# A gated attention trunk: the feed-forward input multiplied by tokens, the residual kept by features

## The chip, the cores and the metric

The kernel runs on one core of a Trainium2 chip. Its five engines work from queues of their own: TensorE (PE in the profile, with PEld for its weight loads), VectorE (DVE), ScalarE (ACT), GpSimd (POOL) and SyncE (SP), which here issues nearly all DMA transfers. The metric is the device time of one execution in microseconds, the median of the runs; smaller is better.

A matmul on TensorE holds one operand of 128 x 128 (the stationary one, `lhsT` in the code) and streams the other (the moving one, `rhs`, up to 512 columns) against it. The profile names a matmul as output <- moving, stationary.

## The reference

Two layers over 512 tokens of 1,024 features, float32. Each adds a gated mixture of a pooling mixer and a differential attention to the residual, and then a SwiGLU feed-forward:

```python
for i in range(DEPTH):                                  # DEPTH = 2
    xn = rmsnorm(x, norm1_g[i])
    u_pool, q, k, v, g_a, g_b = split(xn @ w_in[i])     # 1024 -> 6 x 1024
    q = rotary(rmsnorm(q, q_norm_g[i])); k = rotary(rmsnorm(k, k_norm_g[i]))
    o = diff_attention(q, k, v, lam)                    # softmax(qk, 0) - lam * softmax(qk, 1), chunk-causal
    attn_out = rmsnorm(o, subln_g[i]) * (1 - lam_init)
    pool_out = pool_mixer(u_pool, pool_w[i], pool_scale[i])
    x = x + (sigmoid(g_a) * pool_out + sigmoid(g_b) * attn_out) @ w_out[i]
    hn = rmsnorm(x, norm2_g[i])
    gate, up = split(hn @ w_ffn_in[i])                  # 1024 -> 2 x 2816
    x = x + (silu(gate) * up) @ w_ffn_out[i]            # 2816 -> 1024
```

`rmsnorm(x, g)` is `x * rsqrt(mean(x * x) + 1e-6) * g` over the features of a token.

## The kernel before

**Precision.** Every large product is done in three matmuls. An operand is split into a high part, rounded to the type that TensorE takes, and a low part, the rest; high x high, high x low and low x high are summed in PSUM (`product`, L277 to L285). Weights come in pieces of 512 KB (`piece`, `loaded`) and are split on arrival: a cast on ScalarE (L198) and a subtraction on VectorE (L199). `parts` has a second way: cast, negative copy, and a DMA from memory that adds the weights onto it (L236 to L238, issued by POOL). Raw pieces rotate through 7 buffers, split ones through 6 pairs.

**Layout.** The residual `res` lies by tokens, four tiles of 128 tokens by 1,024 features. A norm (`normed`, L346) squares a tile on ScalarE, raises the mean to the power -1/2 on POOL, scales by it and by the gains on VectorE, and then turns the tile into features by tokens with eight transposes on TensorE (L303); the split of these is the moving or stationary operand of what follows. Layer 0's first norm is different: its input also comes transposed from the host, the products are made of unnormalized `x * g`, and 1/rms is applied behind them (`token_stats`, `spread_rms`). Sums over features are made there with eight small matmuls against a column of ones (L471).

**Mixers.** Four heads, one after the other: query and key, value and gate, then the pooling branch and `merged`, whose last step is a product with the pool weights, two multiplications on VectorE (L750, L751) and a split (L204, L205). Probabilities, queries and outputs are turned by blocks of 32 on VectorE (L310), written to memory by one DMA and read back by four (`turned`, L306 to L316), all on SP's queue. The output projection adds into `res` as heads finish, and the last two heads are projected together (`project_out(..., True)`).

**Feed-forward.** The input product of a pair of hidden tiles, gate and up, 512 columns in all, is made by Strassen's scheme in Winograd's form: the weights are cut into four quarters (half of the features by gate or up), the activations likewise (half of the features by 256 tokens), and seven products replace eight. Sums of weight quarters are made per pair on VectorE (`Ffn.sums`, L816 to L830), sums of activation quarters once per layer (`Quarters`). A product is 24 matmuls (`pair_product`, L287 to L300): weights are held, 256 columns of tokens move. SwiGLU follows by features (`swiglu`). There are 11 pairs in a layer; after 8, 16 and 22 tiles their output product adds into `res` (`ffn_out`), hidden held and weights moving 512 wide, four tiles of tokens by two column blocks.

**Order.** The program is written as one stream. Steps that need a result of another engine are put off by a due time, counted in moving columns (`later`, `run_due`, with the constants `NORM_WAIT`, `QK_AWAY` and so on), and are written into the stream when the matmul count has reached it. The framework's planner then orders each engine's instructions by that stream and by its own estimate of times, hands out buffers by tag, and sets the semaphores; `tc.issue_after` fixes an order by hand.

Of the kernel before, what the change touches and what calls it, by code (L numbers as in the profile page):

```python
# [18 lines left out]
P = 128  # L19
# [20 lines left out]
ROUNDS = ((0, 8), (8, 16), (16, 22))  # L40
# [4 lines left out]
HIDDEN_AT = {0: "u", 2: "m", 4: "pr", 6: "us", 8: "mj", 10: "u", 12: "m", 14: "pr", 16: "us", 18: "u", 20: "m"}  # L45
# [3 lines left out]
QK_AWAY, SCORE_AWAY, PROB_AWAY, AV_AWAY, MERGE_AWAY = 28000, 26000, 32000, 18000, 24000  # L49


def weight_plan():
# [3 lines left out]
    def block(name, layer, cols, k0=0, k1=KD):  # L56
        for k in range(k0, k1, 2):
            plan.append((name, layer, k, 2, cols))
# [12 lines left out]

    for layer in range(L):
        def out(heads):
            for cb in range(2):
                for j in heads:
                    block("w_out", layer, span((512 * cb, 512)), 2 * j, 2 * j + 2)

        for i, j in enumerate(ORDER):
            block("w_in", layer, qk(j))
            if i >= 2:  # L80
                out(ORDER[i - 2:i - 1])
# [4 lines left out]
        out(ORDER[2:])  # L86

        def ffn_in(f, parts):
            cols = span((P * f, 256)), span((FF + P * f, 256))
            for k, up in parts:  # L90
                plan.append(("w_ffn_in", layer, k, 4, cols[up]))

        def ffn_out(f0, f1):
            for cb in range(2):
                block("w_ffn_out", layer, span((512 * cb, 512)), f0, f1)

        for part in ((0, 0), (4, 0)):
            for f in (0, 2):
                ffn_in(f, (part,))
        for r, (f0, f1) in enumerate(ROUNDS):  # L100
            for f in range(f0, f1, 2):
                ffn_in(f, ((0, 0), (0, 1), (4, 1), (4, 0))[1 if f < 4 else 0:3 if f < 4 else 4])
                if r and f == f0:
                    ffn_out(*ROUNDS[r - 1])
        ffn_out(*ROUNDS[-1])
# [4 lines left out]
def trunk_kernel(  # L110
    ctx: ExitStack,
    tc: tile.TileContext,
    x: bass.AP,
# [3 lines left out]
    gains: bass.AP,  # L117
# [31 lines left out]
    stats = const.tile([P, 5, NT], F32, name="stats")  # L149
    mhalf = const.tile([P, 4], F32, name="mhalf")  # L150
    scale = const.tile([P, L * KD + KD], F32, name="scale")
    neglam = [const.tile([P, 1], F32, name=f"nl{i}") for i in range(L)]
    l2s = [const.tile([P, 2], F32, name=f"l2{i}") for i in range(L)]
    const.tile([P, 40], F32, name="pad2")
# [3 lines left out]
    for tag, width, bufs in (("ss", 1, 4), ("r", 4, 4), ("ss4", 4, 4), ("st", 2, 4), ("mx", 2, 4), ("rc", 2, 4), ("sso", 1, 4),  # L158
                             ("head", 16, 2)):
# [3 lines left out]
    res = [sb.tile([P, D], F32, name=f"res{t}", tag=f"res{t}") for t in range(NT)]  # L163
# [43 lines left out]
    def piece(raw=None):  # L207
        i = at[0]
        at[0] += 1
        if raw is None:  # L210
            raw = sb.tile([P, 2, 512], F32, name="raw", tag="raw", bufs=RAWS)
        transfers.append(nc.sync.dma_start(raw.rearrange("p a b -> p (a b)"), wts[i]))
        hi = sb.tile([P, 2, 512], F32R, name="whi", tag="whi", bufs=SPLITS)
        lo = sb.tile([P, 2, 512], F32R, name="wlo", tag="wlo", bufs=SPLITS)
        split(hi, lo, raw)
        return [(hi[:, a, :], lo[:, a, :]) for a in range(2)]

    def loaded():
# [3 lines left out]
        raw = sb.tile([P, 4, VD], F32, name="raw", tag="raw", bufs=RAWS)  # L222
        nc.sync.dma_start(raw.rearrange("p a b -> p (a b)"), wts[i])
        return i, raw

    def tiles(x):
        return [x[:, k, :] for k in range(x.shape[1])]

    def parts(src, piece_no=None):
# [817 lines left out]
```

## Time and profile before

| | |
|---|---|
| median of 3 runs | 1408.1 us (1407.98 to 1408.12) |
| span of the profiled execution | 1406.2 us |
| instructions in it | 21,911, of them 8,140 matmuls |
| DMA | 203.21 MB in 109,979 packets, 145 GB/s on average |
| loads of weight pieces | 244 on SP's queue, 60 more that add onto a split part on POOL's |
| round trips through memory (`turned`) | 84 writes, 336 reads |

The profile is of one execution. A page line gives an engine's busy time, its share of the span and its instructions. A row of the groups view reads: line, engine, operation, output <- inputs, shapes, count | busy us, mean ns of one | idle time of the engine before them and what ended it. A row of the windows view gives for a stretch its length, then busy time and count of each engine, the granted clock and the DMA engines' share and rate. A row of the timeline gives start, duration, engine, line, operation and count of equal neighbours.

### The profile page before, as it was taken

The page shows a single profiled execution, that of the slowest core. Times are in us where ns is not written, and L with a number is a line of the kernel's source. Part 1 is how long each engine was busy: PE and PEld are TensorE (multiplying, and loading weights), DVE is VectorE, ACT ScalarE, POOL GpSimd, SP SyncE. Part 2 cuts the span into 40 slices and gives each one's busy share as a digit, 9 for nine tenths or more (in the row PEclk, how much of TensorE's full clock was granted, in tenths as well). Part 3 has the DMA queues.
Part 4 walks back from the last instruction along what each step waited for, and adds up shares of the span by engine and source line. Part 5 has one row for each costly group of instructions (what it writes and reads, how often), then busy time and mean ns, then how long its engine had stood idle before and what let it go on. Part 6 is the DMA issues. An engine that isn't in the chain of part 4 may idle for free.

```text
span 1406.2 us, 21911 instructions
## 1 busy us (share of the span) xinstructions
PE 1399.6 (100%) x8140; PEld 1237.5 (88%) x8140; DVE 1023.0 (73%) x1923; ACT 688.2 (49%) x1309; POOL 119.0 (8%) x144
## 2 busy tenths in 40 slices
PE   9999999999999999999999999999999999999999
PEld 7888888888999899989888888888889998999897
DVE  7779788697998558737577887767769974676462
ACT  6554343444766346425354543435447662563350
POOL 1010000100000001000010001000010000010000
PEclk9999999999999999999999999999999999999999
DMA  9344453453368357628334445435524682585351
GB/s 363 106 128 136 136 162 122 132 156 103 92 166 225 104 128 187 181 60 236 110 134 151 145 132 175 135 119 155 173 48 127 163 228 68 150 187 158 98 143 60
DMA packets 109979, 203.21 MB, mean 145 GB/s; under 512 B 37424, under 2 KB 62512, under 8 KB 109872
## 3 DMA queue, kind: packets, MB, share of 16 engines
q1 hardware_dynamic: 99936, 168.24, 37.1%
q0 software_dynamic: 8640, 31.46, 12.5%
q10 hardware_dynamic: 1296, 2.11, 0.6%
q8 instruction: 64, 1.05, 0.3%
q14 instruction: 43, 0.35, 0.1%
HBM read 184.07 MB, written 17.69 MB: 143 GB/s over the span
## 4 chain that ended last, share of the span: by engine, by line
PE 97%; DVE 1%; DMA 1%; POOL 0%; issue 0%; ACT 0%; DVEq 0%; SPq 0%; POOLq 0%
PE mm L282 20%; PE mm L284 19%; PE mm L283 19%; PE mm L296 6%; PE mm L294 6%; PE mm L297 6%; PE sc L294 3%; PE sc L297 3%; PE sc L296 3%; PE tr L297 2%; PE tr L294 2%; PE tr L296 2%; PE tr L303 1%; PE sc L284 1%; PE sc L283 1%; PE sc L282 1%
## 5 line engine op out<-in xcount | busy, mean ns | idle before, releaser
L198 ACT CAST whi<-raw 128x1024 fp32r<-128x1024 f32 (+1 forms) x225 | 234.9, 1047 | 200.7 <-issue 84.7
L199 DVE TENSOR_TENSOR wlo<-raw,whi 128x1024 fp32r<-128x1024 f32 (+1 forms) x225 | 271.2, 1213 | 66.4 <-ACT whi L198 64.6
L282 PE MATMUL mm<-whi,xh 128*128 128x512 f32 x480 | 188.7, 393 | 0.0
L284 PE MATMUL mm<-whi,xl 128*128 128x512 f32 x480 | 187.1, 390 | 0.0
L283 PE MATMUL mm<-wlo,xh 128*128 128x512 f32 x480 | 187.1, 390 | 0.0
L760 DVE TENSOR_TENSOR res<-mm,res 128x512 f32<-128x512 f32 (+1 forms) x97 | 65.6, 680 | 113.1 <-PE mm L284 112.9
L284 PE MATMUL mm<-whi,fl 128*128 128x512 f32 (+1 forms) x358 | 138.6, 387 | 0.0
L282 PE MATMUL mm<-whi,fh 128*128 128x512 f32 (+1 forms) x358 | 138.3, 387 | 0.0
L283 PE MATMUL mm<-wlo,fh 128*128 128x512 f32 (+1 forms) x358 | 138.2, 387 | 0.0
L329 POOL TENSOR_TENSOR r<-r,mhalf 128x1 f32<-128x1 f32 (+1 forms) x76 | 64.7, 851 | 615.4 <-DVE r L328 547.5
L284 PEld LDWEIGHTS mm<-whi,xl 128*128 128x128 f32 x480 | 90.1, 188 | 19.2
L283 PEld LDWEIGHTS mm<-wlo,xh 128*128 128x128 f32 x480 | 90.3, 188 | 17.2
L282 PEld LDWEIGHTS mm<-whi,xh 128*128 128x128 f32 x480 | 90.2, 188 | 17.3
L238 POOL DMA_DIRECT2D wlo<-in_wts x60 | 52.6, 876 | 599.4 <-ACT wlo L237 293.1
L282 PE MATMUL mm<-xh,whi 128*128 128x512 f32 x256 | 99.8, 390 | 0.0
L283 PE MATMUL mm<-xl,whi 128*128 128x512 f32 x256 | 99.8, 390 | 0.0
L296 PE MATMUL mm<-xql,whi 128*128 128x256 f32 x352 | 99.7, 283 | 0.0
L294 PE MATMUL mm<-xqh,whi 128*128 128x256 f32 x352 | 99.6, 283 | 0.0
L297 PE MATMUL mm<-xqh,wlo 128*128 128x256 f32 x352 | 99.6, 283 | 0.0
L284 PE MATMUL mm<-xh,wlo 128*128 128x512 f32 x256 | 99.6, 389 | 0.0
L294 PE MATMUL sc<-xqh,whi 128*128 128x256 f32 x320 | 90.7, 283 | 0.0
L297 PE MATMUL mm<-xrh,wlo 128*128 128x256 f32 x320 | 90.6, 283 | 0.0
(243 smaller groups left out, 3506.9 us busy)
## 6 DMA issues: line engine op xcount, KB each, us to landing
raw<-in_wts SPq DMA_DIRECT2D x244, 512.0 KB, 4.4
wlo<-in_wts POOLq DMA_DIRECT2D x60, 512.0 KB, 7.7
away<-near SPq DMA_DIRECT2D x35, 256.0 KB, 2.3
near<-away SPq DMA_DIRECT2D x140, 64.0 KB, 2.1
away<-near SPq DMA_DIRECT2D x35, 128.0 KB, 1.7
near<-away SPq DMA_DIRECT2D x140, 32.0 KB, 2.3
xr<-in_x_t SPq DMA_DIRECT2D x4, 512.0 KB, 7.3
res<-in_x SPq DMA_DIRECT2D x4, 512.0 KB, 8.9
```

What stands on the lines that cost most here:

```text
L198: ins = nc.scalar.copy(hi, src)
L199: nc.vector.tensor_sub(lo, src, hi.bitcast(F32))
L238: nc.gpsimd.dma_start(lo.rearrange("p a b -> p (a b)"), wts[piece_no], accum_op=ALU.add)
L282: nc.tensor.matmul(acc, lhsT=ah, rhs=bh, start=i == 0, stop=False)
L283: nc.tensor.matmul(acc, lhsT=ah, rhs=bl, start=False, stop=False)
L284: nc.tensor.matmul(acc, lhsT=al, rhs=bh, start=False, stop=i == n - 1)
L294: nc.tensor.matmul(acc[:, i, :], lhsT=ah, rhs=bh, start=start and not i and not k, stop=False, skip_group_check=True)
L296: nc.tensor.matmul(acc[:, i, :], lhsT=ah, rhs=bl, start=False, stop=False, skip_group_check=True)
L297: last = nc.tensor.matmul(acc[:, i, :], lhsT=al, rhs=bh, start=False, stop=i == 1 and k == 3, skip_group_check=True)
L303: nc.tensor.transpose(dst, src, ident)
L329: nc.gpsimd.tensor_tensor(r, r, mhalf[:, :width], op=ALU.pow)
L760: added = nc.vector.tensor_add(res[t][:, cs], here, res[t][:, cs])
```

## The change

The input product of feed-forward is turned around. Tokens are held and weights move: a group is now four hidden tiles, its quarters are 512 columns wide (256 of gate, 256 of up), and a product (`multiply`) is 24 matmuls of 512 columns into two banks of 128 tokens each. Five groups make 20 of the 22 tiles; the last pair (`ODD`) is a plain product ahead of them. Weight pieces of 512 KB hold two feature tiles by 512 columns; one quarter (features 4 to 7 of the second pair) is loaded twice per group. Quarters 1, 2 and 4 are split with the DMA that adds, the four sets of sums on ScalarE and VectorE.

Gate and up now come out by tokens. `Hidden.put` makes the activation there, with 1/rms as the scale of a token, and `turned` carries each half of 256 tokens to features by tokens; `back` splits it when it is due. The output product holds weights and moves all 512 tokens of a hidden tile; it is spread over the next group's products (`FILLED`), two feature tiles a time.

The residual lies by features, eight tiles of 128 features by 512 tokens, and so is the output, which the host turns. It starts as the transposed input itself. Norms apply gains per feature (`gain`) and 1/rms behind the products, in both layers and in feed-forward; `normed` and its transposes go. `Sets` makes the activation quarters and their sums. `in_turn` and `chained` fix TensorE's order in feed-forward and in the last projection as written. `square_pair` gathers the squares for `token_stats`, in the two buffers of tag `mj`.

```diff
-ROUNDS = ((0, 8), (8, 16), (16, 22))
+GROUPS = (0, 4, 8, 12, 16)
+PRODUCTS = (1, 5, 6, 2, 7, 4, 3)
+LOADS = {1: ((0, 0),), 5: ((1, 0), (1, 4)), 2: ((0, 4),), 4: ((1, 4),)}
+FILLED = (6, 2, 7, 4)
+ODD = 20
+HIDDEN_AT = {ODD: ("m",), 0: ("mj", "u"), 4: ("pr", "m"), 8: ("mj", "u"), 12: ("pr", "m"), 16: ("mj", "u")}
...
+    def in_turn(acc, pairs, start=True):
+        for i, (a, b) in enumerate(pairs):
+            run_due()
+            with chained() if not i else ExitStack():
+                last = three(acc, a, b, start and not i, i == len(pairs) - 1)
+        chain[0] = last
...
-    def normed(key, t, xh, xl, g, into=None):
...
+    def square_pair(src, n=2):
+        sq = sb.tile([P, 2, S], F32, name="sq", tag="mj", bufs=2)
...
+            for a in range(2):
+                nc.scalar.activation(sq[:, a, :], src[a], AF.Square)
+        if squares[0] is None:
+            squares[0] = sq
+        else:
+            nc.vector.tensor_add(squares[0], squares[0], sq)
...
+        class Sets:
...
+            def put(self, i):
+                g = [gain(2 * layer + 1, d) for d in (i, i + 4)]
+                raw = sb.tile([P, 2, S], F32, name="xg", tag=("u", "pr")[i // 2], bufs=2)
...
+                    nc.scalar.activation(raw[:, a, :], res[i + 4 * a], AF.Copy, scale=g[a])
...
+                    split(hi[a], lo[a], raw[:, a, :])
+                square_pair([res[i], res[i + 4]])
...
+        def last_out(x):
+            for i in range(4):
+                w = piece(4, True)
+                for a in range(2):
+                    acc = mm_ps()
+                    in_turn(acc, [(cols(w, a)[2 * n + h], (ms[j][0][:, h, :], ms[j][1][:, h, :]))
+                                  for n, j in enumerate(ORDER[2:]) for h in range(2)])
+                    add_out(i + 4 * a, acc)
+                x.put(i)
...
+        class Hidden:
...
+            def put(self, half, t, gate, up):
...
+                th = sb.tile([P, VD], F32, name="th", tag="mt", bufs=3)
+                nc.scalar.activation(th, gate, AF.Tanh, scale=stats[0][:, 2, n:n + 1])
+                nc.vector.scalar_tensor_tensor(th, th, 1.0, gate, op0=ALU.add, op1=ALU.mult)
+                nc.vector.scalar_tensor_tensor(
+                    h[:, :, t, :], th.rearrange("p (i c) -> p i c", i=2), stats[0][:, 5, n:n + 1],
+                    up.rearrange("p (i c) -> p i c", i=2), op0=ALU.mult, op1=ALU.mult)
+                if t:
+                    near = turned(h.rearrange("p i t c -> p (i t c)"), 4, ("up", "us")[half], 2)
+                    later(HIDDEN_AWAY, lambda: self.back(half, near))
...
+        def odd_group(x):
...
+            accs = [mm_ps(), mm_ps(), tr_ps(), tr_ps()]
+            for k in range(4):
+                for t in range(NT):
+                    in_turn(accs[t], [((x.xh[:, k + 4 * a, token(t)], x.xl[:, k + 4 * a, token(t)]), w[k][a])
+                                      for a in range(2)], not k)
+                if not k:
+                    x.sums()
+            token_stats(False)
+            for t in range(NT):
+                to.put(t // 2, t % 2, accs[t][:, :VD], accs[t][:, VD:])
...
+        def out_unit(d, w, f0, n, end=False):
+            need(*((layer, f, half) for f in range(f0, f0 + n, 2) for half in range(2)))
...
+                in_turn(into, list(zip(w, moving)))
+                add_out(d, acc, cs)
...
+        def group(g, x):
...
+            a, b, c = [s_ps() for _ in range(2)], None, [tr_ps() for _ in range(2)]
...
+            def multiply(n, to, start=True):
+                xs = x.of(n)
+                for h in range(2):
+                    w = rows_of(sets[n][h])
+                    for t in range(2):
+                        in_turn(to[t], [(tuple(p[:, 2 * h + k, token(t)] for p in xs), w[k]) for k in range(2)],
+                                start and not h)
...
+        def next_x(i):
...
+                nc.scalar.activation(xh[:, d, :], res[d], AF.Copy, scale=g)
+                nc.vector.scalar_tensor_tensor(xl[:, d, :], res[d], g, xh[:, d, :].bitcast(F32), op0=ALU.mult, op1=ALU.subtract)
+            square_pair([res[2 * i], res[2 * i + 1]])
...
+        last_out(sets_of_x)
+        odd_group(sets_of_x)
+        for g in range(len(GROUPS)):
+            group(g, sets_of_x)
+        for i in (2, 3):
+            pair_units(GROUPS[-2], i)
+        for i in range(4):
+            pair_units(GROUPS[-1], i, layer == L - 1)
+            if layer < L - 1:
+                next_x(i)
```

More of the change, by code (lines that the diff above doesn't have):

```diff
@@ L70, in ug, with gate_up @@
         return span((256 * j, 256), (4096 + 256 * j, 256))
+    def gate_up(f):
+        return span((P * f, 256), (FF + P * f, 256))
     for layer in range(L):
[L73 to L76, printed above, removed]
         for i, j in enumerate(ORDER):
@@ L80, in weight_plan @@
             if i >= 2:
-                out(ORDER[i - 2:i - 1])
+                for cb in range(2):
+                    k = 2 * ORDER[i - 2]
+                    block("w_out", layer, span((512 * cb, 512)), k, k + 2)
             block("w_in", layer, vg(j))
@@ L162, in trunk_kernel @@
         sb.tile([P, 4, ROT], F32, name=tag, tag=tag, bufs=2)
-    res = [sb.tile([P, D], F32, name=f"res{t}", tag=f"res{t}") for t in range(NT)]
+    halves = [sb.tile([P, 2, S], F32, name=f"res{i}", tag=f"res{i}") for i in range(KD // 2)]
+    res = [halves[d // 2][:, d % 2, :] for d in range(KD)]
     lams = [sb.tile([P, 2, 2, QK], F32, name="lv", tag="up", bufs=2) for i in range(L)]
@@ L423, in new_xT, with gain @@
+    def gain(i, k):
+        return scale[:, L * KD + i * KD + k:L * KD + i * KD + k + 1]
     def new_xT():
@@ L522, in trunk_kernel, with spread_rms @@
     head_gains(0)
-    ready.update(("x0", t) for t in range(NT))
-    rms_row = sb.tile([P, S], F32, name="rr", tag="hg1")
-    def spread_rms():
+    rms_rows = {}
+    def spread_rms(layer):
         row = tr_ps()
         for t in range(NT):
-            transpose(row[:, token(t)], stats[:, 1, t:t + 1].broadcast_to([P, P]))
-        nc.scalar.copy(rms_row, row)
-    later(81600, spread_rms)
+            transpose(row[:, token(t)], stats[0][:, 1, t:t + 1].broadcast_to([P, P]))
+        rms_rows[layer] = sb.tile([P, S], F32, name="rr", tag=f"hg{1 - layer}")
+        nc.scalar.copy(rms_rows[layer], row)
     for layer in range(L):
@@ L538, in trunk_kernel @@
             head_gains(layer)
+        later(81600, lambda layer=layer: spread_rms(layer))
         def x_tok(t):
@@ L570, in scores @@
                 width = (t + 1) * P
-                prob = []
+                pr = sb.tile([P, 2, S], F32, name="pr", tag="pr", bufs=2)
+                prob = [pr[:, c, :width] for c in range(2)]
                 st = small("st", 2)
@@ L765, in trunk_kernel @@
-        hidden = {}
-        def swiglu(to, h, gate, up):
-            th = sb.tile([P, 2, VD], F32, name="th", tag="tb", bufs=2)
-            nc.scalar.activation(th, gate, AF.Tanh, scale=0.5)
-            nc.vector.scalar_tensor_tensor(th, th, 1.0, gate, op0=ALU.add, op1=ALU.mult)
-            nc.vector.scalar_tensor_tensor(th, th, 0.5, up, op0=ALU.mult, op1=ALU.mult)
-            cs = slice(h * VD, (h + 1) * VD)
-            for i in range(2):
-                split(to[i][0][:, cs], to[i][1][:, cs], th[:, i, :])
```

661 lines of the change are left out of this document (286 added, 375 removed).

## The prediction

> **What bounds the kernel now.** I began with the page: engines, granted clock and the chain of waits.
>
> ```profile
> span 1406.2 us, 21911 instructions
> PE 1399.6 (100%) x8140; PEld 1237.5 (88%) x8140; DVE 1023.0 (73%) x1923; ACT 688.2 (49%) x1309; POOL 119.0 (8%) x144
> PEclk9999999999999999999999999999999999999999
> PE 97%; DVE 1%; DMA 1%; POOL 0%; issue 0%; ACT 0%; DVEq 0%; SPq 0%; POOLq 0%
> ```
>
> TensorE is busy from end to end at full granted clock, and 97% of the chain is its own matmuls. So the time is a count of matmuls times their distance from start to start, and an edit elsewhere counts only if it makes TensorE wait. Durations don't add up to it, because matmuls overlap: the groups view gives 391 ns for a 512-wide matmul and 283 for a 256-wide one, far more than their distance. That I took from the windows view, in a stretch that is all 256-wide products (rows of L294) and one that is all 512-wide feed-forward output (rows of L282, weights moving):
>
> ```profile
> L282 PE MATMUL mm<-whi,fh 128*128 128x512 f32 x346 | 135.0, 391 | 0.0
> L294 PE MATMUL mm<-xqh,whi 128*128 128x256 f32 x352 | 99.6, 283 | 0.0
> ```
>
> ```profile
> core 0: us, PE busy (x) PEld busy (x) DVE busy (x) ACT busy (x) POOL busy (x), PEclk, DMA share, GB/s
> 385.00:455.00 70.00, 70.00 (x586) 70.00 (x585) 62.37 (x82) 45.86 (x65) 6.96 (x8) 1.00 0.77 194
> 465.00:505.00 40.00, 40.00 (x177) 32.91 (x176) 15.76 (x21) 7.94 (x10) 0.87 (x1) 1.00 0.19 43
> ```
>
> With a matmul cut at the edges, 70 us over 584 is 119.9 ns, and 40 us over 176 is 227.3 ns. I use 120 and 227. Two narrow ones cost 240, one wide one 227. In the narrow stretch the weight load is busy throughout and VectorE 89%, and yet TensorE doesn't wait.
>
> **The widths.** The code gives the counts. Before, 11 pairs of hidden tiles per layer each take 7 products of 24 matmuls, 256 wide: 2 x 11 x 168 = 3,696, or 443.5 us. After, five groups of four tiles each take 7 x 24 matmuls of 512 (1,680 in two layers), and the odd pair becomes a plain product of 8 x 4 x 3 = 96 per layer, 192 in all. 1,872 x 0.227 = 424.9 us. That is -18.6, in which giving up the seven-product form for the odd pair costs 192 x 0.227 - 336 x 0.120 = +3.3. If the new ones came at 229 ns, the gain would be 14.8. I take -18: the wide row above has exactly the new form, weights moving and activations held. Output matmuls swap their operands but keep their count and width (22 x 8 x 3 and 8 x 8 x 3 per layer), so they cost nothing new (they stay where they were, on TensorE's path). A hidden tile now moves as two runs of 256 columns, which no row before shows, and I bound that by 0 and by the 2 ns above (+2 us).
>
> The Trainium skill, page "TensorE: Matmul & The Clock Gate", section "Back-to-back issue gap", puts a warm gap at N/2.4 + 2.5 ns: 109.2 and 215.8 ns here. By it the two counts come to 403.6 and 404.0 us, and the widths would buy nothing. This trace disagrees by 11 ns at either width, and the measurement decides.
>
> **The transposes.** The normalization before feed-forward (two layers) and before layer 1 turns its rows on TensorE, 8 transposes per token tile, 12 batches:
>
> ```profile
> 348.79 0.39 PE L284 MATMUL mm<-whi,ml 128*128 128x512 f32 x1
> 349.02 1.03 PE L303 MATMUL tr<-ident,xs 128*128 128x128 f32 x8
> 349.81 0.48 PE L282 MATMUL mm<-whi,mh 128*128 128x512 f32 x1
> 350.12 0.39 PE L283 MATMUL mm<-wlo,mh 128*128 128x512 f32 x1
> ```
>
> 0.79 us of transposes, and the next matmul takes 0.31 instead of 0.23 to its successor: 0.87 x 12 = -10.5 us. In their place `token_stats` runs three more times, and `spread_rms` once more. Their price stands at the start of the trace:
>
> ```profile
> 21.76 0.94 PE L471 MATMUL mm<-ones,sq 128*128 128x1 f32 x8
> 22.56 0.49 PE L513 MATMUL tr<-wlo,xh 128*128 128x512 f32 x1
> 22.89 0.40 PE L514 MATMUL tr<-whi,xl 128*128 128x512 f32 x1
> ...
> 29.29 0.60 PE L303 MATMUL tr<-ident,qn 128*128 128x128 f32 x4
> 29.64 0.48 PE L282 MATMUL mm<-whi,xh 128*128 128x512 f32 x1
> ```
>
> 0.80 + 0.10 = 0.9 us each, 0.43 for four transposes: +3.1 us. Sum on TensorE: -18 - 10.5 + 3.1 = -25.4.
>
> **What must stay hidden.** Layer 1 now multiplies by 1/rms on VectorE, as layer 0 already does without a TensorE wait: nothing. The residual's 4 loads and 6 gain rows go, off the path: nothing. What grows is feed-forward's preparation. VectorE's rows:
>
> ```profile
> L199 DVE TENSOR_TENSOR wlo<-raw,whi 128x1024 fp32r<-128x1024 f32 x223 | 269.8, 1217 | 62.5 <-ACT whi L198 60.7
> L760 DVE TENSOR_TENSOR res<-mm,res 128x512 f32<-128x512 f32 x95 | 64.7, 686 | 109.9 <-PE mm L284 109.8
> L199 DVE TENSOR_TENSOR fl<-th,fh 128x256 fp32r<-128x256 f32 x88 | 32.9, 417 | 0.2
> L310 DVE STREAM_TRANSPOSE near<-qn 128x512 f32<-128x512 f32 x28 | 19.8, 707 | 0.5
> L685 DVE SCALAR_TENSOR_TENSOR vl<-mm,stats,vh 128x256 fp32r<-128x256 f32 x16 | 7.6, 477 | 1.2 <-ACT vh L684 1.0
> ```
>
> A group asks for 8 low parts, 8 sums and 4 output pieces (20 x 1.217), 10 combinations, 8 residual adds and 4 low parts of hidden (22 x 0.686), 8 gates (0.417 + 0.477 each) and 4 transposes (0.707): 49.4 us. TensorE needs 264 x 0.227 = 59.9, so VectorE stands at 82%, below the 89% above. Only group 0, with two output pieces fewer and eight 256-wide splits more (50.3), is asked for more than its 216 x 0.227 = 49.0. Weights: a set's buffers come free about three products (16 us) ahead. The kind with DMA accumulation needs two ScalarE passes, an issue and a landing, which the groups and the DMA table price:
>
> ```profile
> L237 ACT ACTIVATE wlo<-raw 128x1024 fp32r<-128x1024 f32 x60 | 63.3, 1056 | 0.2
> L238 POOL DMA_DIRECT2D wlo<-in_wts x60 | 52.6, 876 | 599.4 <-ACT wlo L237 293.1 <-DVE wlo L199 246.7 <-DVE fl L199 33.6
> ...
> wlo<-in_wts POOLq DMA_DIRECT2D x60, 512.0 KB, 7.7
> ```
>
> 2.1 + 0.9 + 7.7 = 10.7 us. Hidden in the steady state.
>
> **Where TensorE can wait.** (a) `in_turn` puts the closing output units in strict order. After the last mixer product only 9 matmuls (2.0 us) don't need its second half. Before, 54 of them were free to go in any order, which covered this:
>
> ```profile
> 336.34 0.39 PE L284 MATMUL mm<-uh,pwl 128*128 128x512 f32 x1
> ...
> 337.81 0.68 DVE L750 SCALAR_TENSOR_TENSOR ta<-ta,mm 128x512 f32<-128x512 f32 x1
> 338.41 1.22 DVE L817 TENSOR_TENSOR raw<-raw 128x1024 f32<-128x1024 f32 x1
> ...
> 340.15 0.74 DVE L751 SCALAR_TENSOR_TENSOR ta<-ta,scale,mj 128x512 f32<-128x512 f32 x1
> ...
> 340.92 0.63 ACT L204 ACTIVATE mh<-ta 128x512 fp32r<-128x512 f32 x1 [2.36 <-DVE ta L751]
> ...
> 341.94 0.68 DVE L205 SCALAR_TENSOR_TENSOR ml<-ta,mh 128x512 fp32r<-128x512 f32 x1
> ```
>
> The low half came 5.9 us after the product's last matmul, with weight sums in between. Without those it is 0.68 + 0.74 + ScalarE's 0.63 + 0.68 and the hand-overs, about 3 us. Price 1 to 3.9 us per layer; I take 1, since the sums there go. (b) Product 5 of group 0 writes the two banks (`tr`) that token tiles 2 and 3 of the odd pair leave. Before they are free come the statistics' matmuls, their power on POOL and the gates of three tiles:
>
> ```profile
> L475 POOL TENSOR_TENSOR stats<-stats,mhalf 128x4 f32<-128x4 f32 x1 | 1.0, 1038 | 21.7 <-DVE stats L472 21.7
> L687 ACT ACTIVATE tb<-mm,stats 128x256 f32<-128x256 f32 x16 | 7.6, 474 | 13.8 <-DVE vl L685 13.5
> ```
>
> 0.8 + 1.0 + 0.5 + 3 x 0.9 and the hand-overs, about 6 us, against 0.9 + 5.4 of cover (the statistics and product 1). 0 to 4, should the power stand behind a DMA issue that waits for ScalarE (the 293.1 us in POOL's row); I take 0.5. (c) Group 0's VectorE surplus and its last product, whose weights compete with combinations: 0 to 3, I take 0.7. (d) Hidden now goes by token and returns through memory. Its trip in the trace:
>
> ```profile
> 864.35 0.71 DVE L310 STREAM_TRANSPOSE near<-qn 128x512 f32<-128x512 f32 x1
> 865.09 0.33 SPq L311 DMA_DIRECT2D away<-near  x1
> 867.58 1.75 SPq L313 DMA_DIRECT2D near<-away  x4
> ...
> near<-away SPq DMA_DIRECT2D x140, 64.0 KB, 2.1
> ```
>
> From transpose to landing 867.58 + 1.3 + 2.1 - 864.35 = 6.6 us. Combination, tanh and the two gate products before it add 0.69 + 0.47 + 0.42 + 0.48 = 2.1, the two halves of the split behind it 1.3, hand-overs some 0.4: 10.4. Three products cover 16.3, but behind the last group only four output units do, 10.9. 0 to 3, I take 0.8. (e) At the layer's end the squares use the buffers (tag "mj") that the last group's hidden holds until the last unit, so eight squares (0.63 each), three sums (1.22) and a last one (0.69) follow it in turn: 9.4 us and hand-overs, against two products of 24 x 0.227 = 5.4 that layer 1 can do before it needs a bank whose reader waits for the statistics: 0 to 3, once, I take 1. Together 2 x 3 + 1 = 7 us (bounds 2 to 31).
>
> **Sum.** 1406.2 - 25.4 + 7 = 1387.8 for the span; the median of the runs is 1408.1, 1.9 above the profiled span, which I add: 1389.7, rounded to 1389.
>
> **The rivals.** *The waits at their upper ends.* VectorE at over 100% in group 0 and the strict order of (a) speak for it, the 89% without a wait against it. From 13 to 22 of the 31 us: 1382.7 + 13 = 1396 to 1405.
>
> *The SP queue: slower.* 44 more round trips share SP's queue with the weight loads, and there a load that lacks a buffer holds up what stands behind it:
>
> ```profile
> SPq L212 <- DVE wlo L199: 200.9, 58, 17.1
> SPq L313 <- DMA away<-near: 64.4, 49, 2.3
> ```
>
> 3.5 us on average, 17.1 at worst. Output units first meet a group's hidden at 12 places. A delay of d at each costs 10 x (10.4 + d - 16.3) + 2 x (10.4 + d - 10.9) = 12d - 60. It eats the 25.4 from d = 7.1 us on; at 9 us it is 48 and the time 1431. Against it: the attention's trips already share the queue, and the chain gives DMA 1%.
>
> *The widths buy nothing.* The gain rests on a fixed part of each matmul, 2 x 120 - 227 = 13 ns, that is paid half as often. If the wide ones came at 443.5 / 1,872 = 237 ns, because their moving operand is rewritten by VectorE and DMA all the while, nothing would be left of it but the transposes: 1408.1 - 10.5 + 3.1 + 7 = 1407.7, no change. Against it stands the row from 465 to 505, where freshly split weights move. The skill's rule above ends at the same place by another way, a fixed part of only 2.5 ns.
>
> *No waits at all:* 1408.1 - 18.6 - 10.5 + 3.1 = 1382.1, or a little less where old waits go too.
>
> **How the numbers follow.** Forecast (1383 to 1395) 0.70; upper ends 0.18; no waits 0.04; widths nothing 0.03; SP queue 0.05. From 1380 to 1402 it holds over 8 in 10. About 0.2%, 2.8 us, is what a measurement can tell. Faster 0.91, same 0.04, slower 0.05.
>
> **What would show it.** Right: a window inside a group with 264 matmuls in 60 us, no transposes of `xs`, TensorE at 98 to 100% and some 6,240 matmuls; waits only at the layers' joints. Step (a) is right if the first closing unit shows a gap of a microsecond, (d) if the first unit of the last group waits for a low part of hidden, (e) if products of layer 1 stand behind the power of the statistics. Wrong: idle time within groups 1 to 3, a wide distance above 230 ns, or SP with away or near behind waiting loads.

## The result and the profile after

The kernel after takes **1515.97 us** (median of 4 runs, 1509.37 to 1522.68) against 1408.04 before: 1.0767 times as long, 95% interval 1.0735 to 1.0798. It is slower; the prediction (1389, 1380 to 1402) was wrong by 127 us. The profiled execution took 1509.4, with a span of 1507.6.

The page of the kernel after, engines, granted clock and chain of waits:

```profile
span 1507.6 us, 18715 instructions
PE 1414.3 (94%) x6242; PEld 1156.8 (77%) x6242; DVE 1059.6 (70%) x2055; ACT 700.9 (46%) x1310; POOL 129.0 (9%) x151
PEclk9999999998989999999999999999999999999999
PE 64%; DMA 15%; DVE 11%; ACT 4%; issue 3%; SPq 2%; POOL 0%; ACTq 0%; DVEq 0%; POOLq 0%
```

The matmul count is as forecast (6,242 against some 6,240). What is new is that the chain of waits runs through DMA and VectorE for a quarter of the span. The waits view names what TensorE stood for, and where VectorE stood (engine line waited for: us in total, times, longest):

```profile
DVE fl L211 <- ACT fh L210: 67.1, 28, 5.4
PE oy L280 <- ACT fh L210: 62.9, 12, 7.6
```

`fh` is the high part of the hidden that has come back from memory, and L280 with `oy` is the first output unit that reads it. One whole group, from one such wait to the next, and then the stretches around the first of these two waits (windows view, columns as in the prediction):

```profile
545.00:614.20 69.20, 63.32 (x265) 50.99 (x265) 46.08 (x63) 31.32 (x39) 5.20 (x6) 0.94 0.67 183
...
500.00:523.00 23.00, 23.00 (x104) 19.02 (x103) 17.37 (x27) 10.16 (x13) 1.72 (x2) 1.00 0.60 156
523.00:539.50 16.50, 16.47 (x73) 13.23 (x71) 15.10 (x19) 9.47 (x12) 1.66 (x2) 1.00 0.53 154
539.50:545.00 5.50, 0.28 (x2) 0.00 (x0) 2.46 (x4) 2.66 (x4) 0.10 (x1) 0.79 0.99 234
545.00:550.00 5.00, 5.00 (x12) 3.70 (x13) 3.00 (x4) 0.90 (x1) 0.00 (x0) 0.55 1.03 328
550.00:555.00 5.00, 5.00 (x24) 4.13 (x23) 2.50 (x3) 1.05 (x1) 0.00 (x0) 1.00 0.41 166
```

A group has the forecast 264 matmuls, but takes 69 us instead of 60. The last product of the group ends at 523.0, three products of the next group cover 16.5 us, then TensorE stands still for 5.5 us. After it the granted clock is 0.55 for 5 us: 12 matmuls instead of 24. The trip that it waits for, in the timeline:

```profile
530.22 1.22 DVE L867 TENSOR_TENSOR raw<-raw 128x1024 f32<-128x1024 f32 x1
...
532.82 0.70 DVE L314 STREAM_TRANSPOSE near<-h 128x512 f32<-128x512 f32 x1
533.55 0.34 SPq L315 DMA_DIRECT2D away<-near  x1
536.22 1.81 SPq L317 DMA_DIRECT2D near<-away  x4
536.83 0.89 POOL L236 DMA_DIRECT2D wlo<-in_wts  x1 [25.10 <-ACT wlo L235]
538.73 0.87 POOL L236 DMA_DIRECT2D wlo<-in_wts  x1 [1.01 <-PE mm L282]
544.33 0.62 ACT L210 CAST fh<-near 128x512 fp32r<-128x512 f32 x1 [2.34 <-DMA near<-away]
545.00 0.80 PE L280 MATMUL oy<-fh,whi 128*128 128x512 f32 x1 [5.22 <-ACT fh L210]
```

The transposition starts 9.8 us after the product (forecast 2.1), behind splits and sums of weights. The reads are issued by 538.0 and land at 544.3, 6.3 us later (forecast 2.1), while two adding DMAs run and the DMA engines are 99% busy. From product to first matmul that makes 22.0 us, against 10.4 forecast and 16.3 of cover.

Summed over the whole trace, as the excess of each distance between two TensorE starts over 0.227 us (0.120 for narrow matmuls), where it is above 0.25 us: 105.7 us of waits, and 23.3 us in matmuls that came at 427 ns instead of 227. The parts:

| place | us | forecast |
|---|---|---|
| first output unit of ten groups (d) | 58.5 | with the next: 1.6 |
| output units of the last groups (d) | 9.4 | |
| second and third matmul behind such a wait | 10.0 | 0 |
| 427 ns matmuls, low clock | 23.3 | 0 |
| closing projection, both layers (a) | 13.9 | 2 |
| product 5 of a group (b), (c) | 5.2 | 2.4 |
| layers' joint (e) | 3.1 | 1 |

The rest, 5.6, is at the start, in the mixers and, with 1.2, at later output units of group 0. Without all this the span is 1507.6 - 129.0 = 1378.6. Summed the same way, before had 3.7: 1406.2 - 3.7 = 1402.5. So the arithmetic gain was 23.9 us; 25.4 was forecast.

### The profile page after: what moved, and what is told of

Its sections match the earlier page's. It is cut to its first block, busy times and chain, and to the rows that moved or that the text cites. A ratio compares the mean times of both kernels' runs of the same rounds, so it can differ in the third digit from the quotient of the medians.

```text
span 1507.6 us, 18715 instructions
## 1 busy us (share of the span) xinstructions
PE 1414.3 (94%) x6242; PEld 1156.8 (77%) x6242; DVE 1059.6 (70%) x2055; ACT 700.9 (46%) x1310; POOL 129.0 (9%) x151
## 3 DMA queue, kind: packets, MB, share of 16 engines
q0 software_dynamic: 10944, 39.85, 14.4%
## 4 chain that ended last, share of the span: by engine, by line
PE 64%; DMA 15%; DVE 11%; ACT 4%; issue 3%; SPq 2%; POOL 0%; ACTq 0%; DVEq 0%; POOLq 0%
PE mm L299 12%; PE mm L300 12%; PE mm L301 12%; DMA near<-away 8%; DMA away<-near 5%; DMA raw<-in_wts 3%; PE mm L280 3%; PE mm L281 3%; PE mm L282 3%; DVE wlo L211 2%; PE oy L280 2%; PE oy L281 2%; SPq L317 2%; PE oy L282 2%; PE sc L280 2%
## 5 line engine op out<-in xcount | busy, mean ns | idle before, releaser
L280 PE MATMUL oy<-fh,whi 128*128 128x512 f32 (+1 forms) x180 | 80.2, 446 | 65.6 <-ACT fh L210 62.9
L685 DVE TENSOR_TENSOR res<-mm,res 128x512 f32<-128x512 f32 x96 | 65.0, 681 | 53.2 <-PE mm L282 49.0
L333 POOL TENSOR_TENSOR r<-r,mhalf 128x4 f32<-128x4 f32 (+1 forms) x64 | 58.0, 906 | 515.6 <-DVE r L332 442.6
L280 PEld LDWEIGHTS oy<-fh,whi 128*128 128x128 f32 x180 | 38.6, 215 | 79.4 <-ACT fh L210 68.0
L234 ACT CAST whi<-raw 128x1024 fp32r<-128x1024 f32 x76 | 79.3, 1043 | 37.5 <-PE mm L281 35.4
L280 PE MATMUL sc<-whi,xh 128*128 128x512 f32 x240 | 93.6, 390 | 0.0
L282 PE MATMUL sc<-whi,xl 128*128 128x512 f32 x240 | 93.4, 389 | 0.0
L281 PE MATMUL sc<-wlo,xh 128*128 128x512 f32 x240 | 93.4, 389 | 0.0
L235 ACT ACTIVATE wlo<-raw 128x1024 fp32r<-128x1024 f32 x76 | 80.4, 1057 | 25.1 <-PE sc L281 8.6
L281 PE MATMUL oy<-fl,whi 128*128 128x512 f32 (+1 forms) x180 | 79.4, 441 | 0.2 <-DVE fl L211 0.2
```

The lines of the kernel that those rows point to most:

```text
L234: nc.scalar.copy(hi, raw)
L235: nc.scalar.activation(lo, raw, AF.Copy, scale=-1.0)
L280: nc.tensor.matmul(acc, lhsT=ah, rhs=bh, start=start, stop=False, **check)
L281: nc.tensor.matmul(acc, lhsT=ah, rhs=bl, start=False, stop=False, **check)
L282: last = nc.tensor.matmul(acc, lhsT=al, rhs=bh, start=False, stop=stop, **check)
L685: return nc.vector.tensor_add(res[d][:, cs], acc, res[d][:, cs])
```

## The experiments

Unless said otherwise an edit stands alone on the kernel after. Ratios are to the kernel before.

**1. Output units one product later.**

```diff
-FILLED = (6, 2, 7, 4)
+FILLED = (2, 7, 4, 3)
```

> The output units of the group before stand behind products 2, 7, 4 and 3 instead of 6, 2, 7 and 4; nothing is left out. Theory (hidden's way back is late: by 5 to 8 us at each of 10 places, and TensorE runs at 427 ns instead of 227 for some matmuls after each long wait): one product more of cover, 5.4 us, so the ten waits fall from 58.5 us to under 15, the low clock behind them goes too (some 25 us): about 1508 - 45 - 25 = 1440, with 1425 to 1450. Rival (VectorE can't keep up at all, the wait only shows at the first unit): the waits move to the products behind, and the time stays above 1480.

Measured 1470.23, ratio 1.0448 (1.0431 to 1.0466): 46 us won, and a time between the theory's 1425 to 1450 and the rival's 1480. Nearly all waits for `fh` went, but the output units now waited for their banks, whose reader stood on VectorE behind a weight sum, and that for a late load. The waits view of this run:

```profile
DVE raw L860 <- DMA raw<-in_wts: 47.4, 9, 13.6
PE oy L280 <- DVE res L685: 31.7, 11, 5.9
```

**2. Weight sums behind the last transposition.** `turned_by` holds the latest transposition of hidden written before the group.

```diff
+            ahead = turned_by[0]
...
             for n in PRODUCTS:
-                prepare(n)
+                with tc.issue_after(ahead.ins) if n in (5, 6) else ExitStack():
+                    prepare(n)
```

> The weight sums of the next group (products 5 and 6) are put behind the last transpose of this group's hidden on VectorE; nothing is left out. If the lateness arises on VectorE before the trip (the last combinations stood some 5 us behind weight sums): each of the waits shortens by 4 to 6 us, time 1440 to 1465. If it arises in the trip through memory (landing of the four reads 6 us instead of 2): little change, 1490 to 1510, or slower where product 5's weights come late.

Measured 1514.09, 1.0754 (1.0738 to 1.0770): nothing won. The waits for `fh` vanished and the same time came back at product 5, whose weights were now late:

```profile
PE tr L280 <- ACT whi L210: 33.7, 10, 3.9
PE tr L281 <- DVE wlo L211: 17.0, 10, 1.8
```

**3. No trip through memory.** The hidden stays where the transposition left it, so it is in the wrong order.

```diff
-                    near = turned(h.rearrange("p i t c -> p (i t c)"), 4, ("up", "us")[half], 2)
+                    near = sb.tile([P, 4 * P], F32, name="near", tag=("up", "us")[half], bufs=2)
+                    nc.vector.transpose(near.rearrange("p (c k j) -> p k c j", c=4, k=4),
+                                        h.rearrange("p i t c -> p (i t c)").rearrange("p (k c i) -> p k c i", k=4, c=4))
+                    near = near.rearrange("p (q k j) -> p k q j", q=4, k=4)
```

> Leaves out the way of hidden through memory (one write and four reads per half): the blocks of 32 x 32 turned on VectorE are split as they are, so hidden is in the wrong order. If hidden's lateness is the cause of the waits at the output units, all of them go (10.7 us of the 21.8 us from the last product to the split vanish): the ten waits, those of the last group and the low clock behind them, 68 + 33 us: about 1408. What stays is the closing projection (12 us), the joint of the layers (3 us) and product 5 (5 us). If VectorE is short of time, waits of over 20 us stay in the groups: above 1430.

Measured 1415.27, 1.0052 (1.0032 to 1.0072). All waits at the output units went, and 101 us with them. The trip carries nearly the whole loss; what stays is the closing projection, the joint, and a few waits for weights.

**4. No weight sums.** Eight sums per group are left out.

```diff
-                        nc.vector.tensor_add(s1, r21, s1)
...
-                        nc.vector.tensor_sub(r21, r11, r21)
-                        nc.vector.tensor_sub(r11, s1, r11)
...
-                        nc.vector.tensor_sub(r12, r12, s2)
```

> Leaves out the eight sums and differences of weight quarters per group on VectorE (the products take the quarters as loaded): 80 x 1.13 = 90 us less VectorE work. If VectorE makes hidden late, the ten waits shorten by 4 us and more, the time falls to 1440 or below. If the trip through memory does, the waits stay at 5 us and the time above 1490.

Measured 1488.50, 1.0572 (1.0545 to 1.0599). The waits of the closing projection for its bank went, but the ten waits stayed at 4.7 to 6.8 us. A stretch as long as a group of the kernel after, in the windows view of this run, and then its waits:

```profile
545.00:614.20 69.20, 64.01 (x272) 52.24 (x272) 37.70 (x57) 32.33 (x41) 5.73 (x7) 0.95 0.70 185
```

```profile
DVE fl L211 <- ACT fh L210: 116.4, 37, 7.3
PE oy L280 <- ACT fh L210: 59.6, 12, 6.6
```

VectorE has 37.7 us of work in 69.2 instead of 46.1, and what was saved it spends standing at the split (116.4 against 67.1). Less work on VectorE alone does not bring the hidden in time.

**5. The first two together,** and **6. with the joints mended:** the closing projection's residual adds ahead of group 0's sums, the squares in another tag, three pairs of output units behind the last group instead of two (`closing` holds the last residual add of the closing projection).

```diff
-            ahead = turned_by[0]
+            ahead = turned_by[0] if g else closing[0]
...
-            square_pair([res[2 * i], res[2 * i + 1]])
+            square_pair([res[2 * i], res[2 * i + 1]], tag="pr")
...
-        for i in (2, 3):
+        for i in (1, 2, 3):
             pair_units(GROUPS[-2], i)
```

> Both earlier edits at once: output units one product later, and the next group's weight sums behind this group's last transpose. Nothing is left out. Theory (lateness on VectorE before the trip and late landings in it add up to 22 us against 16 of cover): product 5 now comes 5.4 us later behind the last product, so the sums behind the transpose are in time for it, and the waits of both earlier runs go: under 10 us of waits in the groups, 1420 to 1435. Rival (weights, not hidden, are what is late as soon as hidden isn't): waits at products 5 and 6 stay at 3 us and more each, above 1450.

> The run before, and three joints mended: group 0's weight sums stand behind the last residual add of the closing projection (8.6 us in layer 0), the squares at the layer's end use the buffers of tag pr instead of mj (3.1 us), and the last group leaves three pairs of output units behind it instead of two (5 us per layer). Nothing is left out. If these waits have the causes named, 20 to 30 us less than the run before: 1395 to 1410. If they come from DMA or elsewhere, less than 10.

Measured 1502.82, 1.0679 (1.0660 to 1.0698), and 1476.75, 1.0492 (1.0471 to 1.0513). The first missed the theory's 1420 to 1435. The weights were late now, as its rival had it, though less at products 5 and 6 than at the low weights that come by adding DMAs; its waits view:

```profile
PE sc L281 <- DMA wlo<-in_wts: 38.8, 19, 3.6
```

In the second the joint's wait fell from 3.1 to 0.4, the closing projection's 8.6 went, and 26 us were won over the first, within the 20 to 30 expected: (a) and (e) are places of their own, beside the trip.

**7. The trip's reads on ScalarE's queue.**

```diff
-                    near = turned(h.rearrange("p i t c -> p (i t c)"), 4, ("up", "us")[half], 2)
+                    near = turned(h.rearrange("p i t c -> p (i t c)"), 4, ("up", "us")[half], 2, by=nc.scalar)
```

> The kernel after, with the four reads of hidden's trip issued by ScalarE instead of SyncE; nothing is left out. If the 6 to 7 us of landing (2.1 where no weight load is near) come from standing in one queue with 512 KB loads, the landings fall to about 3 us and each of the ten waits shortens by 3 to 4: 1455 to 1475. If it is the DMA engines' common load, landings and waits stay: 1500 to 1515.

Measured 1561.81, 1.1093 (1.1069 to 1.1117), which neither expected. TensorE's waits for `fh` grew to 85.0 us. ScalarE itself was held at the reads: ahead of one tanh it stood 11.6 us, until the reads before it in its queue could go out behind their write. And the reads landed no sooner for having left SP's queue: of four that were issued from 539.1 to 541.0 the last landed only at 552.1, just ahead of the cast of `fh`. So at this place it is not standing in SP's queue that makes them late.

**8. TensorE kept busy.** 24 useless matmuls ahead of each of the ten units.

```diff
+                for i in range(idle):
+                    with chained() if not i else ExitStack():
+                        last = nc.tensor.matmul(acc, lhsT=w[0][0], rhs=sets_of_x.xh[:, 0, :], start=True, stop=True, skip_group_check=True)
```

> The kernel after, with 24 matmuls of no use (5.4 us) ahead of the first output unit of each group but the last, in the same bank; nothing is left out. The waits of 5 to 8 us are filled. If the 427 ns matmuls behind each wait come from TensorE having stood still, they go, at equal or shorter waits: ten times (2.3 + 0.9) us = 30 us less than the kernel after, 1475 to 1490. If they come from something else (DMA, VectorE), no gain: 1505 to 1520.

Measured 1497.22, 1.0634 (1.0602 to 1.0666): 19 us won by adding 240 matmuls (54 us of them), not the 30 expected. The 427 ns matmuls fell from 23.3 to 10.2 us. So the low clock is a result of the standing. With the slow second and third matmul behind each wait it is a cost of its own of some 20 us.

**9. One half of the hidden turned by TensorE.** The last half of each group is transposed by four matmuls against the identity into a `mm` bank, 22,000 columns after its activation, and split from there.

```diff
+            def turn(self, half, h):
+                tp = mm_ps()
+                for i in range(2):
+                    for t in range(2):
+                        transpose(tp[:, (2 * i + t) * P:(2 * i + t + 1) * P], h[:, i, t, :])
+                split(*(x[:, half] for x in self.parts), tp.rearrange("p (i c) -> p i c", i=2))
+                ready.add((layer, self.f0, half))
...
-                        to[0].put(1, t, x2[t][:, :VD], x2[t][:, VD:])
+                        to[0].put(1, t, x2[t][:, :VD], x2[t][:, VD:], True)
```

> The kernel after, in which the half of hidden that product 3 finishes (one of four halves in a group, the last before the next group) is turned by four transposes on TensorE, split from PSUM, instead of through memory; nothing is left out. Theory (this one trip, begun late on VectorE and landing late, is what the first output units wait for): the eight waits of 5 to 7 us in groups 1 to 4 and the low clock behind them go, about 8 x (5.5 + 3) = 68 us, for ten batches of four transposes, 5 us: 1440 to 1455, while group 0's wait for the odd pair's hidden stays. Rival (every trip is as late): the wait passes to the half before, whose trip starts 11 us earlier, and 1490 or more is left.

**10. The same with the joints of experiment 6.**

> The run before, with the joints mended: group 0's weight sums behind the last residual add of the closing projection, the squares at the layer's end in the buffers of tag pr, three pairs of output units behind the last group. Nothing is left out. If the joints' waits (closing projection 11 us, layer joint 3, last group 9, low clock behind them about 8) have these causes, 25 to 30 us less than the run before: 1410 to 1425. It beats the kernel before (1408) only if group 0's waits go too. If DMA bursts make them, 10 us at most.

Measured 1448.09, 1.0283 (1.0267 to 1.0299), and 1423.38, 1.0110 (1.0094 to 1.0127), both as expected. 8 of the ten waits went with one of four halves; the two that stayed belong to group 0, which waits for the odd pair's hidden.

**11. No adding DMAs.** The 76 DMAs that add weights onto a low part are left out; the products lack that part.

```diff
-            nc.gpsimd.dma_start(lo.rearrange("p a b -> p (a b)"), wts[piece_no], accum_op=ALU.add)
```

> The kernel after without the DMAs that add weights onto a split part (76 of 512 KB; those low parts stay the negative weights, so the products are wrong). If these transfers crowd the landing of hidden's reads at the end of a group: landings there fall from 6.5 us to 3 or less, the ten waits from 5.5 us to 2, time near 1460. If the landings stand behind the 512 KB loads of the same queue instead: they stay above 5 us, and the time above 1490.

Measured 1423.45, 1.0110 (1.0090 to 1.0130), 37 us faster than the 1460 that the theory had hoped for. A stretch of one group's length in the windows view of this run, what SP stood for in its waits, and a trip ahead of it in the timeline:

```profile
519.10:579.35 60.25, 60.14 (x265) 49.46 (x266) 45.62 (x63) 31.07 (x39) 0.00 (x0) 1.00 0.51 156
```

```profile
SPq L316 <- DMA away<-near: 94.2, 59, 5.7
```

```profile
506.66 0.70 DVE L313 STREAM_TRANSPOSE near<-h 128x512 f32<-128x512 f32 x1
507.39 0.34 SPq L314 DMA_DIRECT2D away<-near  x1
510.06 1.81 SPq L316 DMA_DIRECT2D near<-away  x4
516.97 0.61 ACT L210 CAST fh<-near 128x512 fp32r<-128x512 f32 x1
```

A group takes 60.25 us with hardly a wait, though VectorE has the same 45.6 us of work in it. The DMA engines are busy 0.51 of it instead of 0.67. In the kernel after, SP stood 142.5 us for the writes of all trips to land before it could issue their reads:

```profile
SPq L317 <- DMA away<-near: 142.5, 62, 7.5
```

VectorE's standing at `fl` fell from 67.1 to 3.1 us. In this run the product ended at 502.2 (the first output unit starts at 518.5, less 16.3). The same transposition, at 506.66, now comes 4.5 us behind it instead of 9.8. Its reads land at 514.9, 8.2 us after it began instead of 11.4. The cast of `fh` comes 2.1 us later still, behind a cast of weights on ScalarE that waits for TensorE, and the trip just fits its cover. At this place, then, 5.3 us of what the adding DMAs cost came by a later VectorE and 3.2 by the last half's own write and reads.

Of the 5.3, most arose in the same way one half earlier. From the second transposition of the group to the third (507.6 to 522.6 and 485.2 to 496.4) VectorE does the same instructions in the same order in both runs, in 15.0 us in the kernel after and 11.2 here. What differs is that in the kernel after it stood at the split of a half whose reads came back late. The kernel after, and then this run:

```profile
520.30 0.62 ACT L210 CAST fh<-near 128x512 fp32r<-128x512 f32 x1 [5.14 <-DMA near<-away]
520.96 0.69 DVE L211 TENSOR_TENSOR fl<-near,fh 128x512 fp32r<-128x512 f32 x1 [4.14 <-ACT fh L210]
522.56 0.70 DVE L314 STREAM_TRANSPOSE near<-h 128x512 f32<-128x512 f32 x1
```

```profile
494.82 0.68 DVE L211 TENSOR_TENSOR fl<-near,fh 128x512 fp32r<-128x512 f32 x1
496.42 0.69 DVE L313 STREAM_TRANSPOSE near<-h 128x512 f32<-128x512 f32 x1
```

**12. The split alone moved.** `back` is put behind the latest transposition on its engine and due later.

```diff
-HIDDEN_AWAY = 22000
+HIDDEN_AWAY = 70000
...
-                split(*(squares_of(x[:, half].rearrange("p i c -> p (i c)").rearrange("p (k c) -> p k c", c=P))
-                        for x in self.parts), near)
+                with tc.issue_after(turned_by[0].ins):
+                    split(*(squares_of(x[:, half].rearrange("p i c -> p (i c)").rearrange("p (k c) -> p k c", c=P)) for x in self.parts), near)
```

> Edit, alone on the changed kernel: the split of a half of the hidden that comes back from memory (fh on ScalarE, fl on VectorE, L211) is put behind the latest 32x32 transposition on its engine, and its due time is raised from 22,000 to 70,000 columns, so that no split stands ahead of the next half's combination and transposition. In the changed kernel VectorE stood still 67.1 us at this split in all (28 times), 5.4 us of it right ahead of the third transposition of a group. Theory now: VectorE is not full there, it stands at the split for the return of the half before, which lands late (8 to 9 us for a read under accumulating DMAs), and so each late return makes the next half's transposition late. Then the last transposition of a group comes some 4 us after the last product instead of 9.6, the eight waits of 5 to 7.7 us at the first output unit in groups 1 to 5 fall to 0 to 2.5, and with the low clock behind them the time goes from 1516 to 1445 to 1470. Rival: VectorE's work, not its standing, makes the transposition late; then the transposition comes as late as before and the time stays within 1% of 1516. Second rival: the standing only moves, to the splits now gathered ahead of the first output unit or to the sets of weights behind them; then the waits come back at products 5 and 6 and the time stays above 1480.

Measured 1523.07, 1.0809 (1.0792 to 1.0825): the theory fell, and the time stayed, as the first rival had it. VectorE's timeline of this run, up to the last transposition of a group whose last product ended at 598.5 (the wait begins at 614.9, less 16.3):

```profile
600.89 1.22 DVE L211 TENSOR_TENSOR wlo<-raw,whi 128x1024 fp32r<-128x1024 f32 x1
...
603.36 1.22 DVE L211 TENSOR_TENSOR wlo<-raw,whi 128x1024 fp32r<-128x1024 f32 x1
...
604.83 1.22 DVE L211 TENSOR_TENSOR wlo<-raw,whi 128x1024 fp32r<-128x1024 f32 x1
605.96 0.48 DVE L784 SCALAR_TENSOR_TENSOR h<-th,stats,cqn 128x256 f32<-128x256 f32 x1
606.48 0.71 DVE L314 STREAM_TRANSPOSE near<-h 128x512 f32<-128x512 f32 x1
```

The place that the split left was filled with weight splits, the transposition still came 8.0 us behind, and the trip behind it took 14.2 (the first matmul came at 620.7) instead of 12.2. Taking this one stand away did not help.

**13. That order on top of experiment 10,** and **14. the odd pair's second half turned by TensorE too.**

```diff
-                to.put(t // 2, t % 2, accs[t][:, :VD], accs[t][:, VD:])
+                to.put(t // 2, t % 2, accs[t][:, :VD], accs[t][:, VD:], t > 1)
```

> Edit: the order of the run before (splits of returned halves behind the latest transposition, due after 70,000 columns) on top of the kernel in which one half per group is turned by TensorE and the joints are mended (1423 us, 1.011 of the kernel before). There VectorE still stands 55.5 us at these splits, and TensorE waits 13.3 us at group 0's first output units and 8.5 us at product 5's and 6's second factor. Theory (standing at the split is what makes the rest late): the waits at products 5 and 6 shrink, 1405 to 1418. Rival (the split's standing costs nothing here, since the half turned by TensorE needs no landing, and the rest is the late reading of group 0): 1419 to 1430.

> Edit: on top of the run before (1414.6 us, 1.0047 of the kernel before) the second half of the odd group's hidden is turned by four TensorE transposes too, and travels through memory no more. What was left there: two waits of 7.3 and 7.2 us, one per layer, ahead of the first output unit that reads the odd group's hidden, with some 3 us each behind them (0.50, 0.37 and 0.55 at the next matmuls, and 512-wide matmuls at 427 ns instead of 227). Theory: these are the last places where a trip through memory is longer than its cover; the first half, 3 us earlier, comes in time. Then the waits fall to 0 to 1.5 each and the time to 1390 to 1402, faster than the kernel before. Rival: the first half is as late (its landing is crowded too), or TensorE waits for the transposes' input; then 1405 to 1416.

Measured 1414.61, 1.0047 (1.0034 to 1.0060), and **1398.29, 0.9942** (0.9928 to 0.9955), both as expected. The last is faster than the kernel before by 0.6%. Its page, and then a stretch inside a layer's groups in its windows view:

```profile
span 1396.0 us, 18691 instructions
PE 1381.3 (99%) x6290; PEld 1142.9 (82%) x6290; DVE 1052.0 (75%) x2043; ACT 698.8 (50%) x1310; POOL 129.5 (9%) x151
PE 88%; DVE 4%; DMA 4%; ACT 2%; issue 1%; POOL 0%; SPq 0%; ACTq 0%; DVEq 0%; POOLq 0%
```

```profile
520.00:580.25 60.25, 60.25 (x269) 49.95 (x268) 45.07 (x62) 30.61 (x38) 5.21 (x6) 1.00 0.73 213
```

TensorE is busy without a break at full clock, adding DMAs included and the DMA engines 73% busy: their crowding costs nothing here once the last half of a group makes no trip. Summed as above, 13.0 us of waits and 1.4 of low clock are left; twelve lots of four transposes take some 5 (0.43 each, by the prediction's row). 1396.0 - 14.4 - 5.2 = 1376.4, near the 1378.6 found for the kernel after.

## Why the prediction was wrong

**TensorE's sum held.** Forecast -25.4, found -23.9 by subtraction. Experiment 14 shows 9.7 us of it as time on the chip, with 14.4 us of waits and low clock and 5.2 of added transposes still in it. The wide matmul came at 227 ns (23.0 us over some 102 between the cut edges), the transposes went, and the rival that the widths buy nothing is excluded. Where TensorE never waited inside feed-forward, a group of 264 took the forecast 60 us.

**Step (d) failed:** a way back of 10.4 us, hidden under 16.3 of cover and priced at 0.8 per layer. It cost 67.9 us of standing, 10 behind it and most of the 23 us of low clock. Two of its terms were mis-sized. The 2.1 between product and transposition counted the instructions that the half itself needs, as if VectorE had nothing else in its order; it was 9.8. Some 4 of these arose where VectorE stood for the return of the half before, so that one late trip made the next begin late. The 2.1 for the reads came from the attention's median, where the queue had no adding DMAs beside it; here 6.3. The hand-overs and the write were near. The step also had no price for the state that follows a wait. And what stood behind it, "VectorE stands at 82%, below the 89% above", was no evidence: a share says nothing of where in a queue one instruction stands. Idle time within groups 1 to 3, which the prediction had named as the sign that it was wrong, is what the trace shows.

**The slower rival had the right place and formula, and a wrong cause and chance.** It named late round trips at the ten units and decided at 7.1 us of delay; the measured trip of 22.0 is a delay of 11.6, and its 12d - 60 gives 79 us for it. But it had the trips standing behind weight loads on SP's queue. The runs show SP standing for the trips' own writes (142.5 us, and 94.2 without adding DMAs). In the kernel after 40 of the 44 writes were issued 0.7 us after their transposition began, and the first read at most 0.4 us after its write had landed. That standing decides nothing by itself either: in experiment 14 it is 175.7. Its chance of 0.05 rested on "the attention's trips already share the queue": those ran with no adding DMA beside them, and how much cover they have was not measured, so they prove nothing for trips with 16.3 under load.

**(a)** had the place, not the cause. The low part's lateness cost 0.8 us in each layer, near the 1 forecast. The 8.6 us in layer 0, and 2.9 in layer 1, came from the bank: group 0's weight sum stood ahead of the residual add on VectorE and waited for a late load, as the timeline of the kernel after shows:

```profile
355.42 1.23 DVE L860 TENSOR_TENSOR raw<-raw 128x1024 f32<-128x1024 f32 x1 [13.41 <-DMA raw<-in_wts]
...
357.17 0.68 DVE L685 TENSOR_TENSOR res<-mm,res 128x512 f32<-128x512 f32 x1
...
357.90 0.79 PE L280 MATMUL mm<-mh,whi 128*128 128x512 f32 x1 [8.46 <-DVE res L685]
```

The prediction had written "since the sums there go": the old sums went, and new ones came to the same place. Experiment 6 removed the wait by order alone. **(b), (c)** came to 5.2 us in both layers, within their bounds, but only 1.5 of it in group 0, where the prediction had put them. **(e)** was right in mechanism, 3.1 us against 1, though TensorE stood at the statistics' own matmuls and not at products behind them; giving the squares another tag left 0.4.

**What holds the trips up.** That the adding DMAs make the trips late is shown (experiment 11). Neither less work on VectorE (4) nor the moved split (12) helped, and the landing times in the traces show why. These are the last trips ahead of the first output units of groups 1 to 4, eight in each run, in us behind the end of the product:

| run | transposition begins | last read lands |
|---|---|---|
| kernel after | 8.2 to 11.2 | 20.9 to 22.4 |
| 4, no weight sums | 6.2 to 7.9 | 20.3 to 22.3 |
| 12, split moved | 6.8 to 9.5 | 20.2 to 25.8 |
| 11, no adding DMAs | 4.5 to 6.8 | 12.3 to 16.0 |

An earlier transposition won nothing, because its reads landed hardly earlier. In the first three rows the last read landed 0.2 to 2.3 us behind an adding DMA, in the kernel after 0.2 to 0.6.

**What stays open.** No run shows by what the adding DMAs hold a read up until then. How much of the 4.5 us that VectorE needs without them is the planner's order was not tested, nor was a run that leaves out both the sums and the stand.

## What to carry to other kernels

A transfer that a change puts on the path has to be priced from the last instruction that makes its data to the first that uses it, with everything that stands in the queues between, and with landing times under the load that will be there. A median from transfers without that load (2.1 us here) was no measure for those under it (6.3). Where the cover was short by a few microseconds, moving an instruction moved the wait, in part in experiments 1 and 5 and wholly in 2 and 12; taking the last trip off the path (9, 10, 13 and 14) brought the gain out.

## What the runs showed of the hardware

A wait of TensorE cost more than its length. Behind the 5.5 us wait the granted clock was 0.55 over 5 us, and 512-wide matmuls came at 427 ns. The number of slow ones hardly depended on the wait: 7 behind one of 2.0 us (experiment 11, ended at 456.4), 8 behind 5.4 and 7 behind 8.6 (the kernel after, ended at 1363.8 and 357.9), while some waits of 1.5 to 3.5 us were followed by none. The Trainium skill, page "TensorE: Matmul & The Clock Gate", section "What's actually happening", has the clock fall to half after an idle window of about 3.4 us. The halving agrees with these traces; the 3.1 us wait at the layers' joint (11 slow matmuls behind it) and the one of 2.0 us show it after less.

The adding DMAs, 76 of 512 KB, landed 8.1 us after their issue, and while two of them and the weight loads ran the DMA engines were 99% busy. Without them the time fell by 92 us, although they move only 40 of the 241 MB and TensorE hardly waited for one of them directly.
